# A hybrid decoder layer on one core: the first block's first two projections are made from raw float32 weights

## The chip, the core and the metric

The kernel runs on one core of a Trainium2 chip. The metric is the device time of one execution in microseconds (us); less is better. In the text PE is TensorE (matrix multiplications), DVE is VectorE, ACT is ScalarE, POOL is GpSimd, and SP is the engine whose queue issues the DMAs.

## The reference

One layer over 4096 tokens of width 1024. The input is normalised, one large projection feeds two groups of heads, and both go through one output projection with a residual add and a final norm:

```python
h = _rmsnorm(x, norm_w)
u = (h @ w_in).astype(f32)
gla_u, rwkv_u = u[..., :GLA_IN], u[..., GLA_IN:]
# GLA: 4 heads of gated linear attention, chunks of 64 ...
shifted_cols = rwkv_u[..., :RWKV_SHIFT_W]
prev = jnp.pad(shifted_cols, ((0, 0), (1, 0), (0, 0)))[:, :-1]
mixed = shifted_cols + (prev - shifted_cols) * rwkv_mu.astype(f32)
r, rk, rv, wl, al = _split(mixed, RWKV_SHIFT_SPLITS)
w = -softplus(-(rwkv_w0 + tanh(wl) @ rwkv_w_up)) - 0.5
a = sigmoid(rwkv_a0 + al @ rwkv_a_up)
kk = (rk * rwkv_k_k) / norm(rk * rwkv_k_k)
# RWKV: 8 heads of 64, S = S * w - (S kk)(kk a) + v k, y = S r, group norm, bonus, silu gate
return x + merged @ w_out          # then the final RMSNorm
```

All inputs and outputs are float32.

## The kernel before

**Tiles.** The 4096 tokens are worked on in 8 blocks of 512 (`TB`), with channels on the 128 partitions. The input projection is cut into 29 weight tiles (`NWT`) of 1024 x 128, 512 KB each in float32. `W_WA` is the tile of the two low-rank inputs (decay and `a`); `W_RK`, `W_R`, `W_RV`, `W_RG` are four tiles each for the RWKV group, one for each pair of heads, and `W_K`, `W_Q`, `W_V`, `W_GG` belong to the GLA group. Eight more tiles make the output projection.

**Split operands.** A projection is not made in float32. Every weight tile is scaled by a power of two (from its largest absolute value) and split into a float16 tile and a float16 remainder; so is the normed x (`x16`, a high and a low part for each of the 8 channel tiles). `proj` sums three products, high times high, high times low and low times high, over 8 channel tiles: 24 steps. A step is two matmuls, one for each half of the 128 output columns (`both`, `duo`). `shift` then takes the bank from PSUM and makes the mix of each token with the one before; the power of two is undone in its factors `mu_s` and `omu_s`.

**The weights' row.** The stream `w` (`stream_w`) goes through all weight tiles in the order of `w_order`: `W_WA`, `W_RK`, `W_R`, `W_K`, `W_Q`, `W_RV`, and so on, and at the end the 8 tiles of the output projection. For each tile ACT takes absolute values with a sum (written over a staging tile, `wo` in the profile), PE and DVE find the maximum over the partitions (`all_max`, tile `amW`), DVE makes the scales from it (`pow2`: tiles `pw`, `scl`, `invs`), and ACT and DVE write the two float16 parts (`split`). The first 20 tiles of the row (`ND`) are split straight into the buffers from which PE reads them in block 0 (`wr`, `wg`) and stored to memory (`wdr`) from there; the later ones go through two staging tiles (`hls`) and memory. From block 1 on all are read back from `wdr`.

**Where the raw tiles lie.** The raw float32 weights have four places, `raws[n % 4]`. They are the memory of `x16` of the odd blocks (both are tile `x` in the profile), so block 1's x can be written only when the row has read its last raw tile. A place is reloaded as soon as its tile is split.

**Block 0's x.** x is loaded into eight float32 tiles (`xfirst`; in the profile `mgg` and `mgr`) in two halves of 256 tokens. In `x_first` PE sums the squares of each half (`stat_t`), DVE makes the inverse root (`newton`: tiles `nva`, `nta`, `nyg`), PE spreads it over the partitions with float32 matmuls against the identity (`spread_t`), DVE multiplies x in place, ACT casts the high part, and DVE or POOL subtracts the low part. With `NHALF = 2` the first two projections of the RWKV stream (`W_WA` and the first `W_RK`) run half by half, so that the first half can begin before the second half's norm is there.

**After that.** From `W_WA` comes the low-rank input (`lora`), from which each pair of heads takes its decay and `a`; from `W_RK` and `W_R` come the operands `DD` and `bk` of a unit (one pair of heads in one block). PE multiplies them into banks, POOL inverts the triangular part, and a serial chain over the chunks (`us`, `uv`, `sv`, `ch`) follows.

**The order.** The program first writes down all instructions as steps with what they depend on. Which step comes when on each engine's queue is then fixed by a long list of ranks, `ORDER`, kept in the file as compressed text; `STARTS` and `COUNTS` steer the order in which buffers are handed out. Nearly every instruction is issued through one helper (line 844) or, for the paired matmuls, another (line 905), so the profile's lines tell little and the tiles' names tell more.

Of the kernel before, what the change touches and what calls it, by code (L numbers as in the profile page):

```python
# [24 lines left out]
P = 128  # L25
# [8 lines left out]
NHALF = 2  # L34
# [35 lines left out]
    "@88n;?Lc<24?R`yG1D=3b+Fs?a~apRbWhoz2Zi%A0{&4SeEit(_;&dBzrtgT!`71XUktxnKst^3BE;4dUb}?+nAPa+15@};gnnm)*Z(K+Z<&KnVNdS`o!0(#F7)Bw;8_<!Hx?h`bgVs}zW}rlICK~*uYU_)d@H^y"  # L70
    "82hOSdcqjk)f;0hEx6uS!V}-_iu^Tl{$`lxFC_4R7KaXzb@(@zU@wR+@OJqAM96wMcQ^P`Gnls=?D)%JV_b~i?j!ac=K8qsxW&W-_K^7sBHnRQSI=>eG2<2;YTxknYvK9(bVb+6r_hP&z`MSW@5Sf;3(z>P-)*8}"
    ")A(l5x)g|Kegyis^1TV*aal9wI;^d%<ArKdbwxC;x?mIDm*7ha3{O)2xe#+d0dbh`fj6m-NXPQk@R)@4e*(|g4H~!l#WNT~H)zatZ{{0ne@~*l!LsQB_!pH|9BJ<NO`2Poo3G*e2PV+#m>PI{9rniWj1TKqLI?OP"
    "6XRo+XZeJ&n*-uGn_@mrz&T&5paT`KexHCHb`;`INj?<WPoECYyBIVq{QLlnVLo2FFt6K`BHo@w+-Thz`+esl@jv9pBX|`ae=zvgXvk!t&#OBlA8al6=zzTA&mO8VR?rW0w10T44A*eK@WUs=_vb*~mawnZ;y(Sz"
    "Zq7LT!2!wMcS+ti#ORJJ5Bq`Fv;8nD{Cg?I>z)BWDS^MVkgSu>&m`UGL6M2@0V&U0NdDr0V!uter~0FHOpV57Zz6i^PwzXh-!%@tocNo>q_%}$`Z4Sy8RNd;`$dMv1NcpDz&t#L&xMvY!DqLS|02m(<k~x<9G^W7"
    "{Z8e;2<YCg;5n|qvwVX1*1MRiH}KgoTDJ_1LD&9Mq<hPGKLK5cKlvV9qm}H@mq~ZEyr6;f*}xI^Kb~U5$8?wXUM?nPnSpM&FXl(Cv8CBt83&Kdf_7}&HGq98&$u7PwJ)A~BaE#8d9J_P0`Yz2`8mWdgA_iQZ@}-q"
    "4`}Bsu?vAQNa6vz;W-K>Za)&=ZwYxW&vg*ZNdWn973N|Tbkn6crwDy?0p>#1|D^DX!=Y<6;yFbRy(#?7>j}K9F2;_RV>_}#Zor<OW-uqRPS=+re`FyhhVEMDI=c5b^4Sl?J$dfrypmuW#HSbD>muk@17d9NHY5MV"
    "-V&KUp$5L*?C>|RjvqjOx*ubU^W7{m`nnu@LVs<*9t+_2zmVdhX~x*(kOeZAzf5@UPlm^3#G`c$N1A7^WXp|m_;q)JO_Vdw^`rN@yTyjMI(&aJ<nJWtx$n_+M915d_Nn;W7X!=S!#^{g{ub=hMZ}9_?`}nU?S;8`"
    "UxC^_Lov?&IPP5?u0uYGG0QpM5C1+iAIWUlyI%<ZUXYJyZ2<YFb<JMDm{srpGGb<9v0j7C{+NvGs6Xn(3OZ=67rLGOPHl~en2UNtE60L=7ipfd*!u<2VSL#AY;y=E<r~<C%i&{DY*QBg*3BHW8PL6QkXvt2{5o*x"
    "TX~X?<Ew}n%k{78F57UTXYYdV{s6rw58KfdyAa>XcVJ`BjM2#&V)kcmj<=xeNSs&JX7}*;F7%@k_Szk0PK#J)#jgaUBMt_=J{$h#Z1Bzn@Ug0YD2a#6cFaqj?958fGaWotu}6zBwl>^%clBYAZ_@g>wg~^bzZAu?"
    ">+ySuyM7<K@-*ndyVZy%NW%VPQ`)!v;fGT_{(Z+B+4!HtV9x{=APe8{;aJ;wgzpibO`E}ZuJf(?AAWl;%`vpf^N0J9ebP<;e!CWaPCufvw_#5zCbM}1jQb^ERfT>x4d1_kwG*HF8#UUSb@1&CFg#SSKilHkhhnb>"  # L80
    "@Ka2IY&r;g^)iZ$)iRb{LV}a|-ouad@b5uRid}OTFf2aF#uvgj%^}f>@8bl&_p!Hj$jzNA#P>7USKo2iAUXIEyAd0>I>nj{hi;UoJ*%;R7RWmLJhNaIs{L6Hztefx&w}^a9H0M)Y^>LS3wSO3V^vofE8I-?>;~Ry"
# [342 lines left out]
def hymba_kernel(ctx, tc, xT, wt, wg, wo, wua, gup, pk, ck, out):  # L424
# [20 lines left out]
    def build(guide):  # L445
# [1512 lines left out]
        def stream_w():  # L1958
# [3 lines left out]
            for n, i in enumerate(o):  # L1962
# [172 lines left out]
```

## Time and profile before

| | |
|---|---|
| median of 3 runs | 2146.33 us (2142.84 to 2146.91) |
| the profiled execution, its own time | 2144.15 us |
| its span, first to last instruction | 2142.4 us |
| busy time of PE, DVE, ACT, POOL | 2092.5, 1615.9, 1274.6, 897.4 us |
| mean granted TensorE clock | 0.996 of full |
| moved by DMA | 322.32 MB, 150 GB/s |

A profile row names the start and the length in us, the engine, the line, the operation, the tile written and the tiles read, the shape, and how many instructions are put together; in brackets stands how long the engine was idle before it, and what ended that. Times count from the span's start. Matmuls overlap, so the length of a row of matmuls holds the tail of the last one; from the start of a row to the start of the next is the better measure.

### The profile page before, as it was taken

Reading aid. Unit: us, or ns where it says so; the run is one execution under the profiler, and the core shown is the slowest. Engines: PE = TensorE matmul, PEld = TensorE weight load, DVE = VectorE, ACT = ScalarE, POOL = GpSimd, SP = SyncE. Lnnn points to the kernel's source line nnn. Section 1 sums busy time; section 2 is a strip of 40 time slices with the busy share of each in tenths; the row PEclk is TensorE's granted clock in tenths of the full one; section 3 lists DMA queues with packets and bytes.
Section 4 is the critical chain, followed back from the end, with each engine's and each line's share of the span. In section 5 each row is a group of like instructions: output and inputs, shape, how many; then the busy total and the mean of one; then the engine's idle time right before and its main releaser. Section 6 shows DMA issues by size and latency. Waiting matters only on the chain.

```text
span 2142.4 us, 69250 instructions
## 1 busy us (share of the span) xinstructions
PE 2092.5 (98%) x27880; PEld 1354.2 (63%) x27880; DVE 1615.9 (75%) x3528; ACT 1274.6 (59%) x3356; POOL 897.4 (42%) x2365
## 2 busy tenths in 40 slices
PE   7999999999999999999999999999999999999997
PEld 5656675666755657557576567656676565755665
DVE  8889988668775787678776776757877478675886
ACT  7678786465644656455755457545575465554562
POOL 3663344561353541636433264442434534335500
PEclk9999999999999999999999999999999999999999
DMA  6758656465344643455534554345634465334442
GB/s 179 226 153 259 215 176 181 133 193 168 93 132 133 198 142 113 122 160 178 148 95 124 175 170 137 100 132 183 178 98 120 132 193 167 109 109 135 143 132 82
DMA packets 273702, 322.32 MB, mean 150 GB/s; under 512 B 129844, under 2 KB 135140, under 8 KB 273380
## 3 DMA queue, kind: packets, MB, share of 16 engines
q1 hardware_dynamic: 273380, 317.89, 49.9%
q8 instruction: 218, 3.57, 0.7%
q14 instruction: 104, 0.85, 0.1%
HBM read 272.74 MB, written 45.05 MB: 148 GB/s over the span
## 4 chain that ended last, share of the span: by engine, by line
PE 77%; DVE 11%; POOL 4%; DMA 2%; issue 2%; ACT 2%; SPq 0%; DVEq 0%; POOLq 0%; ACTq 0%
PE bank L905 61%; PE bank L844 9%; PE ch L905 4%; POOL tm L844 2%; POOL Tc L844 2%; DVE DD L844 2%; PE y L844 1%; PE y L905 1%; DVE bk L844 1%; DVE nva L844 1%; DVE x L844 1%; DVE Nb L844 1%; DVE xr L844 1%; DMA xr<-in_xT_dram 1%; DMA f<-nd 1%
## 5 line engine op out<-in xcount | busy, mean ns | idle before, releaser
L905 PE MATMUL bank<-x,wr 128*64 128x512 f16 (+1 forms) x6732 | 830.1, 378 | 3.2 <-ACT wr L844 1.0
L844 POOL TENSOR_TENSOR tm<-Tc,f 128x60 f32<-128x60 f32 (+24 forms) x961 | 345.6, 360 | 590.0 <-DMA f<-nd 518.4
L905 PEld LDWEIGHTS <-wr 128*64 128x64 f16 x6732 | 367.1, 111 | 256.5 <-issue 17.1
L905 PE MATMUL bank<-x,wg 128*64 128x512 f16 x3180 | 395.6, 380 | 1.1 <-DVE amW L844 0.6
L844 POOL TENSOR_TENSOR Tc<-Tc,tm 128x60 f32<-128x60 f32 (+24 forms) x961 | 345.0, 359 | 74.0
L905 PE MATMUL bank<-x,wo 128*64 128x512 f16 x2760 | 324.8, 379 | 0.2 <-ACT x L844 0.2
L844 POOL TENSOR_TENSOR xacc<-xacc,xr 128x256 f32<-128x256 f32 x196 | 155.0, 815 | 328.7 <-ACT xr L844 200.7
L844 DVE SCALAR_TENSOR_TENSOR sv<-ch,PC,psd 64x64 f32<-64x64 f32 x434 | 122.8, 283 | 215.9 <-PE ch L905 188.0
L905 PEld LDWEIGHTS <-wg 128*64 128x64 f16 x3180 | 173.5, 110 | 131.0 <-issue 3.7
L905 PEld LDWEIGHTS <-wo 128*64 128x64 f16 x2760 | 150.1, 110 | 117.1 <-issue 1.6
L905 PE MATMUL bank<-wg,x 128*64 128x256 f16 x3072 | 197.5, 273 | 0.2 <-DVE qi L844 0.2
L844 ACT COPY us<-ch 64x64 f32<-64x64 f32 x496 | 101.9, 206 | 148.3 <-PE ch L905 126.7
L905 PEld LDWEIGHTS <-x 128*64 128x64 f16 x3216 | 172.8, 110 | 17.5 <-issue 5.0
L844 ACT COPY uv<-ch 64x64 f32<-64x64 f32 x496 | 102.0, 206 | 85.2 <-PE ch L905 78.3
L844 ACT ACTIVATE psd<-sv,PC 128x128 f32<-128x128 f32 x248 | 98.6, 398 | 57.7 <-DVE sv L844 47.6
L844 ACT ACTIVATE sa<-bank,mu_s 128x512 f32<-128x512 f32 x104 | 71.4, 686 | 57.5 <-PE bank L905 50.4
L844 DVE COPY_PREDICATED DD<-mc,bank 64x512 f32<-64x512 uint8 x128 | 93.1, 730 | 4.9 <-PE bank L844 2.6
L844 DVE COPY_PREDICATED Nb<-mc,bank 64x512 f32<-64x512 uint8 x128 | 93.0, 730 | 3.6 <-PE bank L844 1.4
L905 PEld LDWEIGHTS ch<-uv,bk 128*64 128x64 f32 x992 | 67.0, 137 | 40.8 <-ACT uv L844 7.6
L905 PEld LDWEIGHTS ch<-sv,DD 128*64 128x64 f32 x992 | 66.4, 136 | 39.6 <-DVE sv L844 13.3
L905 PEld LDWEIGHTS ch<-us,Nb 128*64 128x64 f32 x992 | 66.2, 137 | 39.8 <-ACT us L844 10.1
L844 PE MATMUL bank<-DD,bk 64*128 64x128 f32 x1024 | 70.9, 283 | 5.7 <-DVE pw L844 2.9
(359 smaller groups left out, 3556.5 us busy)
## 6 DMA issues: line engine op xcount, KB each, us to landing
wr<-wdr SPq DMA_DIRECT2D x254, 256.0 KB
wg<-wdr SPq DMA_DIRECT2D x182, 256.0 KB
xr<-in_xT_dram SPq DMA_DIRECT2D x176, 256.0 KB
wo<-wdr SPq DMA_DIRECT2D x116, 256.0 KB
f<-nd SPq DMA_DIRECT2D x128, 128.0 KB
x<-in_wt_dram SPq DMA_DIRECT2D x29, 512.0 KB
wdr<-wo SPq DMA_DIRECT2D x17, 512.0 KB
rn<-bcda SPq DMA_DIRECT2D x64, 128.0 KB
```

Source lines behind the costliest of these rows:

```text
L844: put(t0, self.name, d, lag, cols, tiles, tab, outs, ins, lambda: f(*a, **kw))
L905: nc.tensor.matmul(x, lhsT=l, rhs=y, start=start, stop=stop)
```

## The change

In block 0 the projections of `W_WA` and of the first `W_RK` no longer go through `proj`. A new function, `proj_raw`, multiplies the raw float32 weight tile with the normed float32 x: 8 steps for each half of the tokens instead of 24. As neither operand is scaled or split, `shift` gets factors without the weight's power of two (`muf`, four columns made on POOL).

The two tiles are therefore skipped where they stood at the head of the row. The reload of the raw places in which they lay waits until both projections are done. They are loaded a second time and split behind the 27 other input tiles and ahead of the output projection's, through the staging tiles and memory; block 1 reads them back like all others. `NHALF` becomes 0. `ORDER`, `STARTS` and `COUNTS` are new, for the whole run.

```diff
-NHALF = 2
+NHALF = 0
...
+        muf = sb(one, [P, 4], F32, "muf")
...
+        RAW = [W_WA, W_RK]
+        raw_done = [0]
+
+        def proj_raw(n, j):
+            raw = raws[n]
+            for m, t in enumerate((pkt, omu)):
+                G.tensor_tensor(muf[:, 2 * n + m:2 * n + m + 1], t[:, j:j + 1], nwx[:, 9:10], ALU.mult)
+            yield after(raw)
+            ps = yield from need("r")
+            for i in range(2):
+                ts = slice(TH * i, TH * i + TH)
+                for k in range(KT):
+                    if i + k > 0:
+                        yield after(xfirst[k][:, ts])
+                    both(ps[:, ts], raw[:, k, :], xfirst[k][:, ts], i + k == 0, i == 1 and k == KT - 1)
+            raw_done[0] += 1
+            return ps
...
-            return o + [NWT + n for n in range(KT)]
+            return RAW + [i for i in o if i not in RAW] + RAW + [NWT + n for n in range(KT)]
...
-        def shift(ps, j, o):
+        def shift(ps, j, o, mu=None):
+            m, om = mu or (mu_s[:, j:j + 1], omu_s[:, j:j + 1])
...
-            rk = shift((yield from proj((yield from get_w(W_RK + p, "r")), xs, "r")), 4 + p, tA("rk"))
+            if u == 0:
+                rk = shift((yield from proj_raw(1, 4)), 4, tA("rk"), (muf[:, 2:3], muf[:, 3:4]))
+            else:
+                rk = shift((yield from proj((yield from get_w(W_RK + p, "r")), xs, "r")), 4 + p, tA("rk"))
...
+                if n < len(RAW):
+                    continue
+                if n == len(RAW):
+                    yield lambda: raw_done[0] == len(RAW)
+                    for k in range(4, 4 + len(RAW)):
+                        load_raw(k, o[k])
...
-                if n + 4 < NWT:
+                if n + 4 < NWT + len(RAW):
                     load_raw(n + 4, o[n + 4])
...
-                WA = shift((yield from proj((yield from get_w(W_WA, "r")), xs, "r")), 12, sb(rt, [P, TB], F32, "v"))
+                if b == 0:
+                    WA = shift((yield from proj_raw(0, 12)), 12, sb(rt, [P, TB], F32, "v"), (muf[:, 0:1], muf[:, 1:2]))
+                else:
+                    WA = shift((yield from proj((yield from get_w(W_WA, "r")), xs, "r")), 12, sb(rt, [P, TB], F32, "v"))
```

More of the change, by code (lines that the diff above doesn't have):

```diff
@@ new lines @@
+    "#xcko&tq<cz9*TZ$Goq@oXOujcMTY;T;m;iPwVeH?$PG>><P00gwB3XYZTync@^51{WTQV{*yUhUfcc3wd$g0Z^s(R-`AS+e`H<{HTU?5c|F9u{tdsGW&Zvd)@gy9V~$VtMc4NS@MyN4dosp$J<+q$;hyG@eKP~k"
+    "yR$jxL38{P`=@~CdlP%44m2{~x{n;At-03w%oKVs$5o}u{WP7{z{kGKB|O(HW(?P048uSp7n)<1`TJYubt|l29mbp|x^2e&<TtID|9i~e-@}}=;XHknITJoP0@n<%#;2NR__`mB^Bd-vjeR56ACGgNwfIIMhDPO@"
+    "!|Ahje0F+@%xLHbO@yH7I;?wu^^!UJkh$Mz%;~n^8+V)IB**^vuIyWDe1jbPye(lYE_xSQ>jqy^x$>xa-3Kx&htHk{KiE0td0VmGkAhF$Z;jcOS+hZZ!q10c?U{GafowelbojmAi0%T&S9$$WFtGbL%MoDi<n?2Y"
@@ new lines @@
+    "=lV|^N8sMQG{;{sZ+>mwzsLN&#Jqk6`)#f{_QE(P&@~!Co8uv$lui!7T3l|epX|jKGwN2eu`fe9WGy$xo?B}Ee%QReYF>{3kN$*tJr}abhpyCw-!{@b-{;Va2I`n%j&GXlUuj;)nq#r~`}-CTA7|0?EYN)1HS1IM"
+    "rO354kh|yObJ>^YL7uzhtPkE{)8w5g>oW%XROqAK`cAI*mihcBk_$p#yFsUQ>7m1{&*y{2gqI%+Jyh2G?NYMLZLV?M-T;lW{`V)$#axVM67k4`WG<lF?O~2B@Vf_6=C6h3+C}p|>GxaEJUwMzzXILxZZjAAL8iP7"
+    "Jx+AD12BehkY53G$~DkeW@24rADwMpFEy`UH^&(4<A8JpIY;>C56$r#^Y{CNpPJXVpwnJZs@_K0E`he|GRPY~hLYU>XUd$9kKwUF20oocW1_#DXkJgo8Xb;t3?+Nubb3y`-Wle+L3l>xZL+5p(mcuh3!nP4IhL9C"
@@ new lines @@
+    "!YCOoC?_%FR98Q%Eg<hP${*PV+bq}cqc!?nub-!I#Sr9UbX#J;j{qEzzn^Ht@eORxMvq2;XFeLEwkhG&F_!o&jwz9H@mnR|A8}$8{oPDlTN*Qeit?);0G^e=s~_(#)0sBVP_82_<Nw<QKik0>T(>4F-%!@S=*C>!"
+    "i?+Eg^EAkyBnLd&=llB?D4w=7ga&({Wl{Us@NbgeXb+(-x14|V258Q{fT>@a|C(^^EPS6BVb2;N{Ck8KD<bUbT<?7i)<otT=D_bcK8xn@?vnpK7XCn@cZa&+INK%;8K=o{d0{jo9pJCaDVtVW<zS>#uAz*L&nY=8"
+    "W2xbw<)oY?r;%%lbKW!Q-^Z`@`TN^$e4ZUwUYa6g>itbymja$?&7LXwb^Y!S(E+1u(Mv44m8PZ43#00KjKaLUXt8It<2^D5q#ZF(Cr9WVUX63d2iXCCBXlmByH_CF@YtBgkX*Z!Q?6Oea>-bQgVn~XbBt;Vv0rH+"
@@ L366 @@
+    "3q7Yv*wy|Y;n5l~"
 )
@@ L445, in build @@
     def build(guide):
-        TABLES = ("pkt", "scl", "invs", "hinv", "mu_s", "omu_s", "carry", "wosc", "woinv", "gnh", "lnh")
+        TABLES = ("pkt", "scl", "invs", "hinv", "mu_s", "omu_s", "carry", "wosc", "woinv", "gnh", "lnh", "muf")
         FINE = {"Nb": 32, "f": 16}
@@ L1326, in proj @@
             return ps
-        def shift(ps, j, o):
+        def shift(ps, j, o, mu=None):
+            m, om = mu or (mu_s[:, j:j + 1], omu_s[:, j:j + 1])
             a = sb(rt, [P, TB + 1], F32, "sa", NSA)
             S.copy(a[:, 0:1], carry[:, j:j + 1])
-            S.activation(a[:, 1:TB + 1], ps, AF.Copy, scale=mu_s[:, j:j + 1])
-            V.scalar_tensor_tensor(o, ps, omu_s[:, j:j + 1], a[:, 0:TB], ALU.mult, ALU.add)
+            S.activation(a[:, 1:TB + 1], ps, AF.Copy, scale=m)
+            V.scalar_tensor_tensor(o, ps, om, a[:, 0:TB], ALU.mult, ALU.add)
             rel("r")
```

602 lines of the change are left out of this document (296 added, 306 removed).

## Prediction

> **What bounds the kernel now.** The first view is the head of the page: the span and the busy time of TensorE (PE).
>
> ```profile
> span 2142.4 us, 69250 instructions
> PE 2092.5 (98%) x27880; PEld 1354.2 (63%) x27880; DVE 1615.9 (75%) x3528; ACT 1274.6 (59%) x3356; POOL 897.4 (42%) x2365
> ```
>
> PE has only 49.9 us without a matmul in the whole span (2142.4 - 2092.5). A change that doesn't take PE work away can gain only from these, or from matmuls that run at a lower clock. So the second view is the table of stretches, which says where they lie. The columns after the stretch and its length: busy us of each engine, granted clock, share of the DMA engines, GB/s.
>
> ```profile
> core 0: us, PE busy (x) PEld busy (x) DVE busy (x) ACT busy (x) POOL busy (x), PEclk, DMA share, GB/s
> 13.00:30.00 17.00, 14.25 (x196) 11.66 (x192) 16.02 (x50) 10.04 (x23) 9.45 (x17) 1.00 0.79 222
> 30.00:46.00 16.00, 12.77 (x156) 8.32 (x150) 14.64 (x55) 14.91 (x27) 2.70 (x4) 0.79 0.39 117
> 46.00:62.00 16.00, 12.30 (x112) 6.32 (x108) 15.87 (x28) 14.46 (x30) 4.21 (x5) 1.00 0.65 214
> 62.00:104.00 42.00, 41.89 (x488) 28.76 (x488) 33.80 (x80) 27.38 (x48) 26.33 (x56) 0.96 0.66 201
> 104.00:160.00 56.00, 50.89 (x658) 31.48 (x659) 47.16 (x110) 41.96 (x102) 36.34 (x105) 1.00 0.55 169
> 160.00:190.00 30.00, 27.83 (x369) 16.79 (x366) 28.86 (x67) 24.13 (x55) 3.07 (x13) 1.00 0.76 240
> 190.00:228.00 38.00, 34.90 (x512) 25.28 (x511) 34.69 (x91) 32.91 (x81) 26.26 (x57) 1.00 0.78 261
> 228.00:270.00 42.00, 42.00 (x544) 24.86 (x542) 38.78 (x90) 29.02 (x66) 7.92 (x20) 1.00 0.71 212
> 2088.00:2142.40 54.40, 43.08 (x616) 28.64 (x610) 36.99 (x102) 15.82 (x46) 2.82 (x4) 0.92 0.26 84
> ```
>
> PE idles 2.75 + 3.23 + 3.70 = 9.68 us between 13 and 62, next to nothing from 62 to 104, 5.11 + 2.17 + 3.10 = 10.38 us from 104 to 228, and nothing from 228 to 270; 11.32 us lie in the last 54 us, which the change doesn't touch. VectorE (DVE) idles 0.98 + 1.36 + 0.13 = 2.47 us of the 49 us up to 62. So the front is bound by DVE, and PE waits there for what DVE makes: split weights, split x, the operands of the first unit. From 62 on PE is the bound wherever the next weight and the next chunk are ready.
>
> The third view is the timeline of PE in the front.
>
> ```profile
> 12.44 1.12 PE L905 MATMUL bank<-ident,nyg 128*64 128x128 f32 x8 [0.95 <-DVE nyg L844]
> 13.34 0.54 PE L905 MATMUL bank<-gtwo,rn 128*64 128x1 f32 x8
> ...
> 20.98 1.12 PE L905 MATMUL bank<-ident,nyg 128*64 128x128 f32 x8 [1.97 <-DVE nyg L844]
> ...
> 32.17 2.24 PE L905 MATMUL bank<-x,wr 128*64 128x256 f16 x38
> 34.24 0.22 PE L905 MATMUL bank<-identb,lrs 128*64 128x128 bf16 x2
> ...
> 41.30 4.69 PE L905 MATMUL bank<-x,wr 128*64 128x512 f16 x24
> ...
> 49.06 4.48 PE L905 MATMUL bank<-x,wg 128*64 128x512 f16 x40
> ...
> 62.11 1.96 PE L844 MATMUL bank<-DD,bk 64*128 64x128 f32 x14 [2.93 <-DVE pw L844]
> ```
>
> At 62.11 PE begins the first unit's score products, having waited 2.93 us; the operands (DD, bk) come from DVE. This instant, when DVE has worked off everything ahead of the first unit, is what the front hands on.
>
> **The change part by part.** *TensorE.* A pair is the two matmuls of one step, on the two halves of the columns. 19 float16 pairs of 256 columns went from 32.17 to 34.24: 0.109 us a pair. The two projections take 2 x 48 such pairs, 10.4 us. In their place stand 2 x 16 float32 pairs of 256 columns. The nearest row is the float32 broadcast at 12.44: 4 pairs of 128 columns until 13.34, 0.225 us a pair, so 0.45 us for 256 columns and 14.4 us in all. PE's work grows by 4.0 us. [...] I take +4.0 us of work and cost it at nothing on the clock, because the 5.98 us that PE idles from 13 to 46 cover it: the first halves can run from about 14, when DVE has the first normed x (the first row of the next fence), since they wait for no weight split. With the second half's statistics between them (eight groups like that at 13.34, some 3 us) the run then ends near 31. Without this cover it would be +4.0 us.
>
> *VectorE, ahead of the first unit.* The splits of the two weights (W_WA and W_RK) leave the front. DVE's timeline has them:
>
> ```profile
> 13.68 0.87 DVE L844 SCALAR_TENSOR_TENSOR mgg<-mgg,nwx,bank 128x256 f32<-128x256 f32 x2 [0.54 <-PE bank L905]
> ...
> 18.40 1.70 DVE L844 SCALAR_TENSOR_TENSOR wr<-x,scl,wr 128x1024 f16<-128x1024 f32 x1
> 20.03 0.56 DVE L844 SCALAR_TENSOR_TENSOR nva<-nva,nta 128x2 f32<-128x2 f32 x1
> ...
> 25.32 0.20 DVE L844 TENSOR_SCALAR invs<-pw,nwx 128x1 f32<-128x1 f32 x1
> 25.45 0.27 DVE L844 TENSOR_REDUCE amW<-bank 128x1 f32<-128x128 f32 x1
> 25.75 0.15 DVE L844 TENSOR_SCALAR pw<-amW 128x1 f32<-128x1 f32 x1
> 25.82 0.65 DVE L844 TENSOR_TENSOR x<-mgg,x 128x256 f16<-128x256 f32 x1
> ...
> 29.30 0.29 DVE L844 TENSOR_REDUCE amW<-bank 128x1 f32<-128x128 f32 x1 [0.34 <-PE bank L905]
> ...
> 29.71 1.28 DVE L844 SCALAR_TENSOR_TENSOR wr<-x,scl,wr 128x1024 f16<-128x1024 f32 x1
> 30.91 0.74 DVE L844 SCALAR_TENSOR_TENSOR v<-bank,omu_s,sa 128x512 f32<-128x512 f32 x1
> ...
> 35.87 0.29 DVE L844 TENSOR_REDUCE amW<-bank 128x1 f32<-128x128 f32 x1 [0.76 <-PE bank L905]
> ```
>
> From start to next start: 18.40 to 20.03 is 1.63 us, 29.71 to 30.91 is 1.20, the scale work at 25.32 to 25.45 is 0.13, at 25.45 to 25.75 is 0.30, and three small operations as at 25.75 are 0.07 each: 3.5 us. The first of them also stood in the middle of the chain that makes the norm of x's second half (nva at 20.03). DVE waits 0.34 and 0.76 us for PE's results at 29.30 and 35.87; with the two projections earlier about half of that goes, 0.5 us. Together the first unit is ready 4.0 us earlier. The ends: 0, if the order written out fills the place with other DVE work, and 4.6 us.
>
> *The weights' row, later.* Each later weight is split two places earlier. Two more rows say where PE waits for want of work:
>
> ```profile
> 176.69 1.70 PE L905 MATMUL bank<-x,wg 128*64 128x512 f16 x14 [0.51 <-DVE wg L844]
> ...
> 219.52 0.34 PE L905 MATMUL ch<-us,Nb 128*64 128x64 f32 x4 [1.24 <-ACT us L844]
> ...
> 223.52 0.34 PE L905 MATMUL ch<-us,Nb 128*64 128x64 f32 x4 [0.36 <-ACT us L844]
> ```
>
> At 176.69 it waits for a split weight; at 219 to 226 it has only the serial chunk chain to run, waits at each of its steps, and a projection that was ready would fill the gaps. The gain lies between 0 and all 10.38 us of 104 to 228. I take the 0.5 us at 176.69 and the 1.24 at 219.52: -1.7 us, the rows nearest to a missing weight.
>
> *The two splits that come back.* They stand at the row's end, which frees the raw tiles in which block 1's x is written:
>
> ```profile
> L844 ACT ACTIVATE wo<-x x29: 1039/1049/1060, 9.3 to 216.8; 128x1024 f32<-128x1024 f32 x29
> ...
> L844 DVE SCALAR_TENSOR_TENSOR wo<-x,scl,wo x9: 1266/1284/1335, 172.2 to 220.6; 128x1024 f16<-128x1024 f32 x9
> ...
> L844 ACT CAST x<-xr x8: 610/618/622, 221.9 to 242.7; 128x512 f16<-128x512 f32 x8
> ```
>
> 29 splits run until 220.6 + 1.3, and block 1's first x follows at 221.9 at once. The count of splits up to there stays 29; their DVE work of 3.5 us comes back. DVE idles 1.14 + 3.31 = 4.45 us from 160 to 228, which covers it, and PE was saturated after 228 with work of block 0. I take +0.5; the ends are 0 and +3.5.
>
> *The rest.* The two extra reads of 512 KB are about 2 us each at 250 GB/s (an estimate from the rates of 160 to 228), with the DMA engines 0.76 to 0.78 busy: nothing. One issue on the DMA queue waits longer: the load into the first raw tile, which now needs PE to have read it.
>
> ```profile
> 24.02 0.42 SPq L844 DMA_DIRECT2D x<-in_wt_dram  x1
> ...
> 39.77 1.04 ACT L844 ACTIVATE wo<-x 128x1024 f32<-128x1024 f32 x1
> ```
>
> It was issued at 24.02 and its tile read at 39.77. By the estimate above the second projection ends near 31, and the first, 3.6 us of half a projection earlier, near 27; so both reloads have 8 us or more of room; what may be queued behind them is setup for the gate path, which isn't what the first unit waits for. Four 1-column multiplications on GpSimd lie in its idle time before the shift: nothing. NHALF counts only the two projections that are replaced: nothing.
>
> *Sum.* -4.0 - 1.7 + 0.5 = -5.2 us: 2144.15 for the profiled execution becomes about 2139. That execution lies 2.2 us under the median of the runs shown, so against 2146.33 I forecast 2141.1 us, 0.24% less. About 0.2%, 4.3 us, is what a measurement of this kernel can tell from no change.
>
> **The rivals.** *A: DVE keeps its sum.* DVE does the same work ahead of block 1's x as before, only in another order. If the deferred 3.5 us are not covered, the -4.0 of the front is given back before 228 and the later waits stay: -0.5, 2145.8 us. For it: DVE is 0.96 busy from 160 to 190 and 0.91 from 190 to 228. Against it: its 8.2 and 8.8 us of idle time in 62 to 104 and 104 to 160, into which an advanced row can move.
>
> *B: slower, the row's pace.* The last nine splits have 48.4 us between the first and the last, 6.05 us each, far over their DVE work: the row runs beside other work and shares two staging tiles. If the two returned splits take 6.05 us each at the end and the front of the row moves up only 4.0, block 1's x starts 8.1 us later. Once PE runs out of block 0's work it idles for it: 2146.33 + 8.1 = 2154.4 us. It decides as soon as the last split ends some 4.3 us later than before, beyond 226. Against it: 42 us of PE work without a gap after 228.
>
> *C: PE is what the front waits for.* The clock was granted at 0.79 in 30 to 46, 3.4 us of PE time lost; 12 pairs took 4.69 us at 41.30, 20 pairs 4.48 us at 49.06. If an unbroken run of float32 passes keeps the clock up and the whole front follows PE, 9.68 + 3.4 - 4.0 = 9.1 us come in, and with the later 1.7 and 0.5 the gain is 10.3 us: 2136.0. Against it: DVE's 2.47 us of idle time up to 62. [...]
>
> **How the numbers follow.** The forecast has 0.50, and 0.37 of it is a gain over 0.2%; A has 0.25, B 0.15, C 0.10. Faster: 0.37 + 0.10 = 0.47. Same: 0.13 + 0.25 = 0.38. Slower: 0.15. The likeliest case alone lies between 2136 (a few us more of the 10.38 filled) and 2144 (front gain halved). The range reaches below C for a further 3 us of filled gaps, to 2133, and above A to half of B, 2150.
>
> **What would show it.** Right: float32 pairs of x and raw weights from about 14 to 31 at 0.43 to 0.45 us; no wr split on DVE before 20; the first score products at about 58 instead of 62.11; less PE idle time than 10.38 us between there and 228; the last wo split still ending near 220. Wrong: float32 passes set ahead of the second half's statistics, so that the broadcast of its norm comes later than the 20.98 of now; the first score products at 62 or later; a PE gap after 228 while block 1's x is being made; or a new order that opens gaps in the long middle, of which no row here says anything.

## Result and profile after

The changed kernel takes 2164.12 us (median of 4 runs, 2157.85 to 2164.84); the kernel before, timed beside it, 2146.62 us (4 runs, 2142.84 to 2148.36). The ratio is 1.0084, 95% interval 1.0071 to 1.0097: slower by about 17.5 us, where 2141.1 and a range up to 2150 were forecast. The profiled execution is the fastest of the four, 2157.85 us; against the 2144.15 of before it shows 13.7 us of the 17.5, and the rest isn't seen in a trace. Of the 13.7, 5.7 are more busy time of PE (2098.2 us against 2092.5) and 8.0 more idle time (57.9 against 49.9). One execution of e10 below, of 2607.73 us at a mean clock of 0.782, counts in its median and not in its ratio.

The head of the page of the changed kernel, and its table of stretches (columns as in the table of before):

```profile
span 2156.1 us, 69126 instructions
...
PE 2098.2 (97%) x27816; PEld 1354.5 (63%) x27816; DVE 1608.5 (75%) x3528; ACT 1275.6 (59%) x3356; POOL 894.0 (41%) x2369
```

```profile
13.00:30.00 17.00, 12.91 (x124) 8.48 (x122) 11.73 (x37) 8.88 (x25) 7.19 (x15) 1.00 0.59 175
30.00:46.00 16.00, 15.77 (x144) 8.34 (x146) 11.57 (x50) 11.33 (x20) 0.80 (x3) 0.89 0.44 136
46.00:62.00 16.00, 11.34 (x98) 5.36 (x96) 15.57 (x34) 14.39 (x28) 3.17 (x4) 0.89 0.48 154
62.00:104.00 42.00, 41.39 (x500) 27.63 (x496) 35.10 (x85) 29.90 (x55) 28.46 (x60) 1.00 0.69 219
104.00:160.00 56.00, 51.93 (x661) 32.79 (x662) 47.86 (x110) 42.75 (x103) 36.31 (x108) 0.97 0.53 162
160.00:190.00 30.00, 28.24 (x372) 18.36 (x370) 28.77 (x72) 24.71 (x54) 2.13 (x10) 1.00 0.81 252
190.00:228.00 38.00, 35.59 (x560) 26.66 (x558) 32.53 (x85) 34.38 (x86) 21.17 (x50) 1.00 0.87 281
228.00:270.00 42.00, 31.23 (x362) 18.28 (x358) 34.25 (x76) 20.25 (x42) 10.71 (x32) 0.84 0.56 173
```

DVE is relieved in the front as meant: from 13 to 62 it is busy 38.87 us instead of 46.53, and idles 10.13 us where it idled 2.47. Nothing came of it, as the front timeline below shows. From 104 to 228 PE idles 8.24 us instead of 10.38. The lost idle time stands in one row: from 228 to 270 PE worked through all 42.00 us before; now it works 31.23, at a clock of 0.84. PE, SP, DVE and ACT rows of that stretch:

```profile
237.59 0.37 SPq L844 DMA_DIRECT2D td<-Tc  x1
238.74 1.38 SPq L844 DMA_DIRECT2D xr<-in_xT_dram  x3
241.94 0.75 DVE L844 SCALAR_TENSOR_TENSOR xr<-xr,nwx,xacc 128x512 f32<-128x512 f32 x1 [5.48 <-DMA xr<-in_xT_dram]
242.73 0.62 ACT L844 CAST x<-xr 128x512 f16<-128x512 f32 x1 [5.61 <-DVE xr L844]
247.65 0.65 PE L844 MATMUL bank<-ki,gtwo 128*32 128x128 f32 x8 [8.16 <-ACT ki L844]
251.63 3.36 PE L844 MATMUL bank<-DD,bk 64*128 64x128 f32 x28 [2.61 <-DVE DD L844]
```

PE stands still for 8.16 and 2.61 us, while block 1's x is being made (xr is its raw form). The weights' row and that x, in the groups of their tiles:

```profile
L844 ACT ACTIVATE wo<-x x29: 1040/1054/1070, 30.1 to 225.5; 128x1024 f32<-128x1024 f32 x29
L844 DVE SCALAR_TENSOR_TENSOR wo<-x,scl,wo x11: 1264/1279/1343, 172.2 to 242.6; 128x1024 f16<-128x1024 f32 x11
L844 ACT CAST x<-xr x8: 617/618/619, 232.4 to 256.3; 128x512 f16<-128x512 f32 x8
```

The last split starts at 242.6 instead of 220.6, block 1's first x at 232.4 instead of 221.9, its last at 256.3 instead of 242.7. The place is that of rival B, but not all of the waits are. The ninth split and the first of the two returned ones on DVE (the second is the one at 242.6):

```profile
219.78 1.28 DVE L844 SCALAR_TENSOR_TENSOR wo<-x,scl,wo 128x1024 f16<-128x1024 f32 x1
...
229.16 1.26 DVE L844 SCALAR_TENSOR_TENSOR wo<-x,scl,wo 128x1024 f16<-128x1024 f32 x1
```

ACT had made the first part of the last split by 236.6; its second part stood on DVE's queue behind the x at 241.94, which waited 5.48 us for its load. So the row's end waits for x here as well as x for the row. Nor does all of x need the row's last raw tile: each raw place is the memory of two of x's eight tiles. In the kernel before the last raw tile lay under the first two; with two more tiles in the row it lies under the fifth and sixth, which are cast at 245.25 and 246.44, after the last split. Three tiles are cast before it.

The front: PE's timeline, then three rows of DVE's, and the row of before (last) that answers to the third of them:

```profile
13.99 1.10 PE L905 MATMUL bank<-mgg,x 128*64 128x256 f32 x4
14.87 0.33 PE L905 MATMUL bank<-gtwo,r 128*64 128x1 f32 x4
...
17.83 1.95 PE L905 MATMUL bank<-mgg,x 128*64 128x256 f32 x8
19.57 1.68 PE L905 MATMUL bank<-mgr,x 128*64 128x256 f32 x12
...
22.27 2.38 PE L905 MATMUL bank<-mgg,x 128*64 128x256 f32 x20 [0.59 <-DVE mgg L844]
24.48 1.47 PE L905 MATMUL bank<-mgr,x 128*64 128x256 f32 x12
27.66 0.25 PE L905 MATMUL bank<-identb,amW 128*64 128x128 bf16 x2 [1.71 <-DVE v L844]
29.47 0.24 PE L905 MATMUL bank<-identb,amW 128*64 128x128 bf16 x2 [1.57 <-DVE amW L844]
...
30.10 3.59 PE L905 MATMUL bank<-mgg,x 128*64 128x256 f32 x16 [0.33 <-DVE amW L844]
33.62 1.48 PE L844 MATMUL bank<-x,wgs 128*32 128x512 f16 x24
...
40.80 0.22 PE L905 MATMUL bank<-identb,amW 128*64 128x128 bf16 x2
...
63.79 1.61 PE L844 MATMUL bank<-DD,bk 64*128 64x128 f32 x24 [0.61 <-DVE pw L844]
```

```profile
26.85 0.75 DVE L844 SCALAR_TENSOR_TENSOR v<-bank,muf,sa 128x512 f32<-128x512 f32 x1 [1.89 <-ACT sa L844]
...
35.37 0.42 DVE L844 TENSOR_REDUCE amW<-f 128x1 f32<-128x256 f32 x1 [2.79 <-DMA f<-in_gup_dram]
...
41.76 1.27 DVE L844 SCALAR_TENSOR_TENSOR wr<-x,scl,wr 128x1024 f16<-128x1024 f32 x1
```

```profile
42.09 1.28 DVE L844 SCALAR_TENSOR_TENSOR wr<-x,scl,wr 128x1024 f16<-128x1024 f32 x1
```

The W_WA projection is done at about 25.8 and its mix (v) follows at 26.85, 4 us earlier than the 30.91 of before. But the second raw projection runs only from 30.10 to 40.8, behind two maxima of the setup (amW) that PE waited for. W_R, the third weight of the row before and the first that is split now, has its second part made at 41.76, where it was 42.09. Its group of absolute values begins at 30.1, where the row before began at 9.3. The row didn't move up, and the first score products came at 63.79, 1.7 us later than before. What fell behind is the setup: the first of the two maxima, ready on DVE at 16.16 (15.65 before), was taken up by PE only at 27.66 when v was made (16.30 before). The split of the gate weight that hangs on it moved from 20.51 to 29.33, the eight loads that follow (f from in_gup) were issued by 33.94 instead of 27.24, and DVE waited 2.79 us for them at 35.37.

### The profile page after: what moved, and what is told of

It is laid out like the page before. It is cut to its first block, busy times and chain, and to the rows that moved or that the text cites. A ratio compares the mean times of both kernels' runs of the same rounds, so it can differ in the third digit from the quotient of the medians.

```text
span 2156.1 us, 69126 instructions
## 1 busy us (share of the span) xinstructions
PE 2098.2 (97%) x27816; PEld 1354.5 (63%) x27816; DVE 1608.5 (75%) x3528; ACT 1275.6 (59%) x3356; POOL 894.0 (41%) x2369
## 4 chain that ended last, share of the span: by engine, by line
PE 75%; DVE 10%; POOL 5%; DMA 3%; ACT 3%; issue 2%; SPq 1%; DVEq 0%; POOLq 0%; ACTq 0%
PE bank L905 59%; PE bank L844 9%; PE ch L905 4%; POOL Tc L844 2%; POOL tm L844 2%; DVE DD L844 1%; PE y L844 1%; PE y L905 1%; DMA xr<-in_xT_dram 1%; SPq L844 1%; DVE bk L844 1%; DVE x L844 1%; DVE xr L844 1%; DVE nva L844 1%; DMA f<-nd 1%
## 5 line engine op out<-in xcount | busy, mean ns | idle before, releaser
L905 PE MATMUL bank<-x,wr 128*64 128x512 f16 x6540 | 815.6, 380 | 2.3 <-DVE Nb L844 0.8
L844 POOL TENSOR_TENSOR tm<-Tc,f 128x60 f32<-128x60 f32 (+24 forms) x961 | 339.2, 353 | 605.0 <-DMA f<-nd 533.8
L905 PEld LDWEIGHTS <-wr 128*64 128x64 f16 x6540 | 354.9, 110 | 253.1 <-issue 13.8
L844 POOL TENSOR_TENSOR Tc<-Tc,tm 128x60 f32<-128x60 f32 (+24 forms) x961 | 352.1, 366 | 74.2
```

The costliest lines, as they stand in the source:

```text
L844: put(t0, self.name, d, lag, cols, tiles, tab, outs, ins, lambda: f(*a, **kw))
L905: nc.tensor.matmul(x, lhsT=l, rhs=y, start=start, stop=stop)
```

## The experiments

Theories at the start. **R**: the returned splits lengthen the weights' row, so that block 1's x is late. **O**: the new order as a whole is poorer. **H**: on SP's queue the store of Tc (the triangular inverse that POOL makes) waits for POOL and holds up the loads of block 1's x behind it (the rows at 237.59 and 238.74 above). **F** came later: the raw front itself costs the time.

**First group: one part of the change, the rest of the given order kept.** Each step takes its rank from its fellow in the order that it is derived from.

e1 leaves the return out of the changed kernel:

```diff
-  return RAW + [i for i in o if i not in RAW] + RAW + [NWT + n for n in range(KT)]
+  return RAW + [i for i in o if i not in RAW] + [NWT + n for n in range(KT)]
-                D.dma_start(w[a], wdr[i][a])
+                D.dma_start(w[a], wdr[W_R if i in RAW else i][a])
...
```

> The changed kernel without the two returned tiles: they are not loaded and split a second time, and from block 1 on the two projections read the stored tile of the first W_R in their place (this part of the result is left out; PE's, DVE's and the reads' work from block 1 on stay the same). Order inherited from the changed kernel. Theory R (the returned splits lengthen the weights' row, and block 1's x comes later): 2145 to 2151 us, the first CAST of block 1's x near 222 instead of 232. Rival O (the new order as a whole costs the time): 2158 or more. Rival H (the DMA queue standing behind the store of a triangular inverse costs it): 2155 or more, since that store stays where it is.

Measured 2172.23 us, ratio to before 1.0130 (1.0115 to 1.0145): slower than with the return. R's bound is missed; those of O and H hold.

e2 keeps the kernel before and adds the return alone:

```diff
-  return o + [NWT + n for n in range(KT)]
+  return o + [W_WA, W_RK] + [NWT + n for n in range(KT)]
...
```

> The kernel before with one part of the change alone: its front stays as it was, and the two tiles W_WA and the first W_RK are loaded a second time and split again behind the 29 input tiles. Order inherited from the kernel before, the new steps put where their neighbours stand. R: 2155 to 2165 us, 9 to 18 over before, and block 1's first CAST 10 us later than 221.9. O and H: within 4 us of before, 2143 to 2151, since DVE's 4.45 us of idle time from 160 to 228 cover the work.

Measured 2172.36 us, 1.0132 (1.0115 to 1.0149), 27.6 us over before and beyond all bounds. Block 1's x in e1 and e2:

```profile
L829 ACT CAST x<-xr x8: 617/618/619, 242.8 to 270.8; 128x512 f16<-128x512 f32 x8
```

```profile
L830 ACT CAST x<-xr x8: 613/618/619, 236.9 to 267.4; 128x512 f16<-128x512 f32 x8
```

In both x ends 11 us or more after the 256.3 of the changed kernel, and both are slower; but e1 has two splits fewer, so it isn't the number of splits that delays it there.

e3 was to move, in SP's queue of the changed kernel, the store of Tc behind the four loads that follow it (ranks alone, no line of code).

> The changed kernel, with only the DMA queue's order changed at one place: the store of the triangular inverse (td) that waits for POOL until 237 is put behind the four loads that now stand after it (one wg load, three loads of block 1's x). H: the PE gap of 8 us at 239 goes and the time falls by 8 us or more, to 2156 or less. R: those loads wait for x's staging tiles until 234 to 236 anyway, so 3 us at most come back: 2161 to 2164.

Measured 2162.46 us, 1.0084 (1.0068 to 1.0099): the changed kernel's own ratio. But SP's queue did not change there; in e3's trace the store still stands ahead of the loads:

```profile
240.96 0.37 SPq L837 DMA_DIRECT2D td<-Tc  x1
...
242.01 1.37 SPq L837 DMA_DIRECT2D xr<-in_xT_dram  x3
```

A rank takes effect only among steps whose dependences are already written down. So e3 says nothing on H, and in the given order H stays untested. It can hold the loads by 3 to 5 us at most: the last steps of DVE on the three staging tiles of x end at 233.7, 235.0 and 235.8, and the loads were issued from 238.74 on.

e4 gives the changed kernel the ranks and the buffer guide of the kernel before.

> The changed kernel with the ranks and buffer guide of the kernel before, the new steps put where their neighbours stand. O: 2140 to 2149 us, at or under before. R: 2156 to 2166, as the returned splits lie at the row's end in this order too.

Measured 2197.28 us, 1.0245 (1.0228 to 1.0262). None of the theories had that. With an order taken over from other steps these three are 27 to 53 us over before, and e1 is 10 us over e3, which is the changed kernel in all but rank numbers, although work is taken away. So parts can be compared only under an order written for each.

**Second group: an order written anew for each.** The kernel's file holds a planner (forward and backward over the steps, by its own table of costs). It wrote a new order for each of four kernels, followed here by a stage of random small moves.

e5 and e6 are the kernel before and the changed kernel with new ranks and no other edit; e7 is e1's edit, e8 is e2's.

> The kernel before, nothing changed but the order: the ranks are written anew by the program's own planner, from its costs, by one procedure that is used in the same way for the next three kernels. Only differences between these four count. The level is open: 2145 to 2160 us. It is the base of the four.

Measured 2181.10 us, 1.0169 (1.0152 to 1.0186), over the 2145 to 2160 that were expected of its level.

> The changed kernel, the order written anew by the same procedure. R (the two returned splits lengthen the weights' row and hold up block 1's x, in any order): 8 to 16 us over the kernel before with a new order. O (the changed kernel's own order was only a poor one): within 4 us of it.

Measured 2195.11 us, 1.0240 (1.0219 to 1.0261).

> The changed kernel without the two late loads and splits (block 1 on reads the tile of the first W_R in their place), the order written anew by the same procedure. R: back to the kernel before with a new order, within 5 us; if the raw front itself is worth the predicted 4 us, 4 us under it. O: no difference to the changed kernel with a new order (under 4 us). F (the raw front itself costs the time): as slow as the changed kernel with a new order, 8 us or more over before's.

Measured 2175.47 us, 1.0146 (1.0131 to 1.0161).

> The kernel before with its split front kept, and the first two tiles loaded and split once more at the end of the input weights' row, the order written anew by the same procedure. R: 8 to 16 us over the kernel before with a new order, as the changed kernel. F and O: within 4 us of the kernel before with a new order.

Measured 2192.92 us, 1.0221 (1.0195 to 1.0247).

The whole change costs 14.0 us (e6 - e5), without the return it costs nothing (e7 - e5 = -5.6), and the return alone costs 11.8 in the kernel before (e8 - e5). R's bounds hold in e6 and e8, and e7 is 0.6 beyond R's 5; O's and F's fail. The price stands here, but the path to it isn't seen: the last cast of block 1's x starts at 266.6 in e5, 270.4 in e6, 261.8 in e7 and 262.3 in e8, so e8 has its x earlier than e5. Nor do the traces hold the whole price: e8's is that of the fastest of four executions (2182.64 to 2196.21) and only 1.6 us over e5's.

**Third group: what of the return costs.** These orders come from the planner alone, without the random moves. Their expectations speak of one procedure with e5 to e8; that was not so, and their level against those four says nothing. e13 to e15 are their bases.

e13, e14, e15 and e17 are e5, e6, e7 and e8 again, with planner-only orders.

> The kernel before with an order from the planner alone. The orders of e5 to e8 had, behind the planner, a stage of random small moves that e9 to e12 did not have, so the two sets can't be compared with each other; this run and the next two are the bases of the second set. Level open, 2153 to 2165 us.

Measured 2154.56 us, 1.0033 (1.0023 to 1.0044).

> The changed kernel with an order from the planner alone. R (the two returned splits at the row's end cost the time, in any order): 8 to 16 us over e13, and 8 us or more over e9 (2165.8), e11 (2156.1) and e12 (2163.5). O (a poor order of the changed kernel): within 4 us of e13.

Measured 2183.61 us, 1.0168 (1.0150 to 1.0185).

> The changed kernel without the two late loads and splits (block 1 on reads the tile of the first W_R in their place), order from the planner alone. R: within 5 us of e13, and as e11 (2156.1), which has the loads and not the splits. If the raw front itself saves the 4 us that were predicted: 4 us under e13, with the first score products earlier than there. F (the raw front costs the time): 8 us over e13.

Measured 2162.99 us, 1.0070 (1.0052 to 1.0087).

> The kernel before, its split front kept, and the first two tiles loaded and split once more at the end of the input weights' row; order from the planner alone. Base: e13, 2154.6. R (the returned splits cost the time, whatever the front): first cast of block 1's x near 240 us instead of 219, and 15 to 28 us over e13, 2170 to 2183. F (the raw front costs it): 2153 to 2159.

Measured 2183.50 us, 1.0164 (1.0133 to 1.0195).

The return alone costs 28.9 us (e17 - e13) and the change 29.1 (e14 - e13), where R allowed 28 and 16. The change without the return costs 8.4 (e15 - e13), over R's 5 and on F's bound of 8. The DVE group of the row in e13, e14, e15 and e17, in this order (block 1's x is in the table below):

```profile
L862 DVE SCALAR_TENSOR_TENSOR wo<-x,scl,wo x9: 1258/1283/1322, 172.3 to 221.3; 128x1024 f16<-128x1024 f32 x9
L860 DVE SCALAR_TENSOR_TENSOR wo<-x,scl,wo x11: 1259/1283/1285, 173.7 to 249.8; 128x1024 f16<-128x1024 f32 x11
L854 DVE SCALAR_TENSOR_TENSOR wo<-x,scl,wo x9: 1260/1280/1285, 178.1 to 225.8; 128x1024 f16<-128x1024 f32 x9
L854 DVE SCALAR_TENSOR_TENSOR wo<-x,scl,wo x11: 1260/1284/1364, 177.5 to 247.2; 128x1024 f16<-128x1024 f32 x11
```

Two more splits move the end of the row by 24.0 us with the raw front (225.8 to 249.8) and by 25.9 with the split front (221.3 to 247.2), and block 1's x comes later with it, by 16.3 and 23.8 us at its first cast. With the return x starts 4 to 6 us ahead of the last split and ends behind it.

e10 keeps the two splits and drops their loads (they read what lies in the raw places, other tiles); e11 keeps the loads and drops the splits:

```diff
e10
-                if n + 4 < NWT + len(RAW):
+                if n + 4 < NWT:
e11
+                if n >= NWT and i in RAW:
+                    continue
```

> The changed kernel without the two late loads: the two returned splits are made from what lies in the raw places (other tiles, so block 1 on gets wrong factors for these two). The order written anew by the same procedure. If the splits cost and not the loads: as the changed kernel with a new order, 2190 to 2200. If the loads and their queue cost: 2174 to 2183.

Measured 2182.60 us, 1.0159 (1.0129 to 1.0188): e14 without a difference.

> The changed kernel with the two late loads into the raw places and without their splits (block 1 on reads the tile of the first W_R in their place). The order written anew by the same procedure. If the splits cost: as the kernel without the return, 2171 to 2180. If the loads cost: 2188 to 2200.

Measured 2156.07 us, 1.0049 (1.0030 to 1.0068), 27.5 us under e14; x from 222.1 to 241.5. Read as written, e10 lies in the range for the loads and e11 under both of its ranges, but these were written for the level of e5 to e8. Against their own base the two are clear: the splits cost, the loads don't. e11 also gives a scale: it is e15 with two loads more and is 6.9 us faster. So much can the order alone make, and F's 8.4 in e15 (1.5 in e11, -5.6 in e7) is not beyond it.

e12 brings the two tiles back behind 14 others instead of behind 27:

```diff
-  return RAW + [i for i in o if i not in RAW] + RAW + [...]
+  o = [i for i in o if i not in RAW]
+  return RAW + o[:14] + RAW + o[14:] + [...]
```

> The changed kernel; the two tiles come back behind 14 of the 27 other input tiles instead of behind all 27, through the same staging tiles. The order written anew by the same procedure. The count of splits ahead of block 1's x is the same 29. If a split anywhere ahead of block 1's x costs the same (the row as a sum): no gain, 2190 to 2200. If the place counts (late, where DVE and ACT are full and x follows at once): 6 to 14 us under 2195, 2181 to 2189.

Measured 2163.48 us, 1.0074 (1.0053 to 1.0094): 20.1 us under e14 and as e15, with the same 29 splits ahead of block 1's x. Split in the middle of the row, the two cost nothing that shows; split at its end they do.

e9 and e16 free block 1's x from the end of the row: the returned tiles are loaded, half and half, into two tiles that are idle in block 0, and x is written down ahead of them:

```diff
+            raw = spare                      # two idle tiles of 128 x 512
+            for h in range(2):
+                D.dma_start(raw[h]..., wt[i][:, 4 * h:4 * h + 4])
...
-  ... and done["W"] >= NWT)
+  ... and done["W"] >= NWT - 2)
```

> The changed kernel; the two returned tiles are loaded one after the other into two tiles that lie idle in block 0 (half a weight each) instead of the memory of block 1's x, are split there in halves, and block 1's x is written down ahead of them; the order written anew by the procedure of the four kernels before. The returned work is all there (4 more instructions on ACT and 4 on DVE, 2 smaller loads more). R1 (block 1's x has to wait for the end of the row): first cast of block 1's x back near 232 us instead of 248, and 8 to 16 us under the changed kernel with a new order (2195), so 2178 to 2188. R2 (the returned splits simply take engine time that was full): no gain, 2192 to 2202.

Measured 2165.83 us, 1.0090 (1.0069 to 1.0111), 17.8 under e14; x from 223.7 to 248.6. (The factor that undoes the power of two of the two tiles lacks the scale of x there, so block 1 on gets wrong values of the same shape.)

> As e9, with two other idle tiles in which the returned tiles lie, and the factor that undoes the power of two of these tiles as in the changed kernel (in e9 it lacked the scale of x). R1 (block 1's x waits for the row's end): near e13, 8 us or more under e14. R2 (the splits' engine time): as e14.

Measured 2177.03 us, 1.0141 (1.0124 to 1.0158), 6.6 under e14 and 22.5 over e13; x from 232.2 to 256.6. That is on R1's side, but short of its 8 us: the row's own nine splits end at 229.9 there (221.6 in e9), and x is late with them. e9 and e16 are nearly one kernel and lie 11.2 us apart, again the scale of what orders make; the 20 to 29 us of this group lie beyond it, the 11.8 and 14.0 of the second group hardly.

The ten planner-only kernels, by the last cast of block 1's x (starts in us, from the group of that cast in each). They ran in three sessions; the kernel before, timed beside them, took 2146.86, 2147.60 and 2147.25 us:

| kernel | first cast | last cast | median, us |
|---|---|---|---|
| e13 before | 219.3 | 241.5 | 2154.56 |
| e11 loads without splits | 222.1 | 241.5 | 2156.07 |
| e18 quarter of float32, no return | 222.0 | 246.3 | 2160.92 |
| e9 late tiles aside | 223.7 | 248.6 | 2165.83 |
| e12 return after 14 | 226.3 | 249.5 | 2163.48 |
| e15 no return | 227.2 | 250.4 | 2162.99 |
| e16 late tiles aside, 2 | 232.2 | 256.6 | 2177.03 |
| e10 splits without loads | 241.7 | 260.0 | 2182.60 |
| e17 before plus return | 243.1 | 261.4 | 2183.50 |
| e14 changed kernel | 243.5 | 263.6 | 2183.61 |

A straight line through them rises 1.4 us per us of the last cast, and none is more than 4 us off it. A wait for x alone would give 1, so the late cast goes along with more than it causes. The four of the second group do not lie on such a line, as said.

Why does the row end 24 to 26 us later for two splits of 1.28 us on DVE? Only half of that lies at the returned splits. The ninth split, the last that is not a returned one, already starts 10.5 us later in e14 than in e15 (236.31 against 225.84) and 13.8 later in e17 than in e13 (235.15 against 221.31). The two returned ones follow in 13.5 and 12.1 us, 6.0 to 6.8 each: the pace that the row had before the change, 6.05. Rows of e14, engine by engine:

```profile
220.22 1.06 ACT L860 ACTIVATE wo<-x 128x1024 f32<-128x1024 f32 x1 [1.48 <-DMA wdr<-wo]
...
244.06 1.05 ACT L860 ACTIVATE wo<-x 128x1024 f32<-128x1024 f32 x1
...
248.04 1.15 ACT L860 ACTIVATE wo<-x,scl 128x1024 f16<-128x1024 f32 x1
```

```profile
223.85 0.76 DVE L860 SCALAR_TENSOR_TENSOR rn<-rk,pkt,rn 128x512 f32<-128x512 f32 x1 [5.54 <-DMA rn<-bcda]
...
228.93 1.28 DVE L860 SCALAR_TENSOR_TENSOR wo<-x,scl,wo 128x1024 f16<-128x1024 f32 x1
...
236.31 1.27 DVE L860 SCALAR_TENSOR_TENSOR wo<-x,scl,wo 128x1024 f16<-128x1024 f32 x1
...
241.56 1.28 DVE L860 SCALAR_TENSOR_TENSOR wo<-x,scl,wo 128x1024 f16<-128x1024 f32 x1 [1.19 <-ACT wo L860]
246.09 0.28 DVE L860 TENSOR_REDUCE amW<-bank 128x1 f32<-128x128 f32 x1
...
249.82 1.28 DVE L860 SCALAR_TENSOR_TENSOR wo<-x,scl,wo 128x1024 f16<-128x1024 f32 x1
```

The delay ahead of the ninth: the seventh split starts at 211.91 and the eighth at 228.93, 17.0 us later. Its maximum came on PE at 222.92, behind 12.1 us of one projection that PE had begun at 211.01, and DVE then waited 5.54 us for a load. In all five kernels of the two groups with the return at the end, 11.5 to 17.0 us lie between these two splits, in the others 7.7 to 11.0; why the orders come out so isn't shown.

The last split: from the absolute values (ACT, 244.06) by the maximum (PE 245.26, DVE 246.09) and the first part (ACT, 248.04) to the end of the second (DVE, 251.1) it is 7.0 us over three engines, in turns; a split may only begin when a staging tile is free, and at 220.22 ACT waited 1.48 us for such a store. From the second part of the split before to this one's is 8.3 us. DVE wasn't full: the row of the table from 190 to 228 in e14, then in e13:

```profile
190.00:228.00 38.00, 32.88 (x402) 23.56 (x404) 23.80 (x64) 26.87 (x64) 23.98 (x65) 0.87 0.72 235
```

```profile
190.00:228.00 38.00, 34.09 (x490) 24.40 (x486) 31.95 (x79) 31.10 (x74) 25.62 (x55) 1.00 0.79 254
```

DVE idles 14.2 us there in e14 and 6.05 in e13, and 4.5 of the 42 us from 228 to 270, where e14's returned splits lie. So engine time as a sum (R2) doesn't explain the price, and e12, with the same splits at another place, says the same. What fits is a row that goes in turns over three engines with fixed queues, and x behind its end; this path is argued from the rows, and no run tests it alone. H has no part here: in e14 the store of Tc (230.91) is issued 14 us ahead of the loads of x (245.22).

**The front.** e18 is e15 with the float32 passes cut to a quarter:

```diff
-                for k in range(KT):
+                for k in range(6, KT):
...
```

> e15 (the changed kernel without the return, 2163.0) with the raw projections cut to the last two of their eight steps: 8 float32 pairs instead of 32, the other channel tiles left out of these two projections in block 0. Order from the planner alone. P (the float32 passes hold the front back): first score products 6 us or more earlier than the 71.09 of e15, near the 59.5 of e13, and 4 us or more under e15. C (the front is a chain of statistics, norm, setup and the third weight's split, in which the passes only fill PE): first score products within 4 us of 71, and within 4 us of e15.

Measured 2160.92 us, 1.0065 (1.0044 to 1.0086), 2.1 under e15, which its interval can't tell from none. First score products in e13, e15 and e18:

```profile
59.48 2.06 PE L862 MATMUL bank<-DD,bk 64*128 64x128 f32 x32 [0.49 <-DVE pw L862]
```

```profile
71.09 2.06 PE L854 MATMUL bank<-DD,bk 64*128 64x128 f32 x32 [0.90 <-DVE pw L854]
```

```profile
65.98 2.06 PE L854 MATMUL bank<-DD,bk 64*128 64x128 f32 x32 [1.68 <-DVE bk L854]
```

The raw front of e15 hands on 11.6 us later than the split front of e13. Taking 24 of 32 pairs away gives 5.1 of these back, between the bounds of P and C, while the time is on C's side. So the passes seem to be a part of it; that the chain around them is the rest is not tested. The first score products start at 63.79 to 71.09 in the changed kernel and the raw fronts of e6 to e18, and at 59.48 to 62.11 in the kernel before and the split fronts of e5 to e17; none of the versions beat the kernel before.

## Why the prediction was wrong

**The returned splits: the step that failed.** "I take +0.5; the ends are 0 and +3.5." The step priced two splits by DVE's busy time and covered them with its idle time. In two sets of orders the return alone, and the change against the change without it, cost 11.8 and 19.6 us (second group) and 28.9 and 20.6 us (third). In the third group the two took 6.0 to 6.8 us each from start to start, where 1.3 us of DVE had been counted, and the row ahead of them and block 1's x came later too. In the given order the last split came 22.0 us later and x 10.5 to 13.6 us later; PE lost 10.77 us from 228 to 270. "PE was saturated after 228 with work of block 0" was true, but that work ends before the late x is there.

**Rival B** named place, mechanism and the point of decision (last split beyond 226; it was 242.6). Its price was too low by one term: it let the front of the row move up by 4.0, and the front stood still. Without that term two splits at 6.05 us are 12.1 us, inside the 10.5 to 13.6 by which x came later, and B would have read 2158.4. That the sizes agree is partly luck: from start to start the two took 9.4 and 13.5 us, and the second of them stood behind x's own load. It got 0.15 because "42 us of PE work without a gap after 228" was read as cover; that cover had an end.

**VectorE ahead of the first unit**, -4.0: wrong in sign, +1.7. The relief itself is there (7.7 us less DVE work from 13 to 62, of which 3.5 had been counted; some of it, as two steps of bk, lies only later), but DVE's sum doesn't set the instant. W_R's split, the next one needed, stayed at 41.8 while the setup fell some 9 us behind (29.33 against 20.51), so the freed time became idle time. What alone held that split isn't shown. The forecast's own lower end, "0, if the order written out fills the place with other DVE work", was too high as well: the place was filled with nothing.

**TensorE**, +4.0 us of work at no cost: the row at 12.44 was misread. In the trace of the changed kernel a float32 matmul has two records (128 for the 64 matmuls of the two projections), so the 8 records at 12.44 are two pairs of 128 columns of 0.45 us each, not four of 0.225. A pair of 256 columns took 0.88 us in some rows (13.99 to 14.87, two from 17.83 to 19.57, four from 30.10 to 33.62) and 0.44 in another (five from 22.27 to 24.48); with these seven slow ones alone the 32 pairs take 17.2 us, not 14.4. The lower end of the "0.43 to 0.45 us" that were to show the forecast right was the author's estimate; no row of before shows it. Over the whole span PE's busy time grew by 5.7 us. Nor did the run end near 31, but at 40.8: "the 5.98 us that PE idles from 13 to 46" were not there to be filled, since the second projection stood behind PE's waits at 27.66 and 29.47, and 4.32 us of them are idle still.

**The later row**, -1.7: PE idles 2.1 us less from 104 to 228, so the size holds, by luck: the reason given, splits two places earlier, doesn't hold, as the first staged split starts at 172.2 in both kernels. What filled the gaps was not tried.

**The rest.** The two loads cost nothing, as said (e11, 2156.07 us, against the 2162.99 of e15). "A new order that opens gaps in the long middle" has not come: of the 1818 us from 270 to 2088 PE is busy 1807.96 before and 1807.22 after.

What stays open: how the 17.5 us divide between x's wait for the row, the store of Tc (H), the longer work of PE and the given order as a whole (the trace holds 13.7 of them), and why the same two splits cost 12 us in one set of orders and 29 in another.

## What to carry to other kernels

A step that returns to the end of a chain is priced by the chain's pace, start to start (6 to 7 us here), not by an engine's busy time (1.3 us), and one asks what waits for the chain's end. Relieving the busiest engine of a stretch gained nothing here (7.7 us less DVE work from 13 to 62, the first score products 1.7 us later), as the next instruction that the path needs didn't move: find that one first. With a written-out order, compare parts only under orders written anew in one way for each, with a base of their own, and take the difference between two nearly equal kernels (7 to 11 us here) as the least that counts. When an edit changes only ranks, look in the trace whether the queue changed.

## What the hardware showed

In the changed kernel float32 pairs of 256 columns ran at 0.88 us at 13.99 and 17.83 and again at 30.10 (four from there to 33.62), behind waits of 1.71 and 1.57 us, and at 0.44 us from 22.27 to 24.48: two durations a factor of 2.0 apart. For the four from 30.10 on the granted clock reads 0.54 (to 31.90) and 0.50 (from 31.90 to 33.62), and 1.00 from 22.27 to 24.48, which fits the factor. For the pairs at 13.99 and 17.83 it reads 1.00 as well, so the column doesn't show their longer time; what made them slow isn't shown.
